# The first loads of a decoder layer spread over three DMA queues, and two of the first products exchanged

## The chip, the cores and the metric

The kernel runs on one core of one Trainium2 chip. The metric is the device time of one execution in microseconds, as the median of several runs.

## The reference

One layer of a decoder trunk works on x of 256 positions by 1024 channels, in float32. Cut to what matters here:

```python
h = rmsnorm(x, norm1_g)
u = einsum('bsd,de->bse', h, w_in)
x_rnn, g_rnn, q, k, v, g_br = split(u)        # 1024 columns each, g_br has 2048
ya = rg_lru(causal_dwconv(x_rnn)) * gelu(g_rnn)
yb = attention(rmsnorm(q), rmsnorm(k), v)     # 8 heads of 128, causal
x  = x + (sigmoid(gA) * (ya @ w_proj_rnn) + sigmoid(gB) * (yb @ w_proj_attn)) @ w_out
h  = rmsnorm(x, norm2_g)
x  = x + (gelu(causal_dwconv3(h @ w_up)) * (h @ w_gate)) @ w_down
```

The change touches only the beginning: the loads of x and of the columns of `w_in` that make k, and the first of the products x · w.

## The kernel before

Every float32 operand is split into a high part in the format that TensorE multiplies at full rate (fp32r) and a low part that holds the rest, and every product is made of three: high·high, high·low and low·high. ScalarE makes the high part (a cast for weights; for x an activation that also multiplies by the norm's factor g, tile `g1`), VectorE the low part (a subtraction). So nothing can be multiplied before its load has landed, ScalarE has cast it and, for the low parts, VectorE has subtracted.

TensorE works through units: `k` first, then `rx`, `rg`, `ri`, `q` and so on to `w_down`. In unit `k` the sum runs over eight slices of 128 channels, k = 0 to 7. For each slice there are two halves of 512 output columns, g = 0 and 1, and for each half three pairs of matmuls (a pair is the two halves of the 256 positions). So a slice is six pairs. Nine small matmuls on a tile of ones (`warm`) run before the first of them.

The first operands come in small pieces. `load_x(a, b)` loads slices a to b of x transposed into `xT` (128 KB a slice). `load_w(k, g)` loads 128 channels by 512 columns of weights into `raws` (256 KB). In the text x0, x1, x23 are the pieces of x for slice 0, slice 1 and slices 2 and 3, and w0.1 is the weight piece of slice 0, half 1. A piece of `raws` gives `his` and `los`; a slice of `xT` gives `xgh` and `xgl`. In unit `k`, SyncE's queue carries all pieces of x and of weights; ScalarE's queue carries only `g1`, of 4 KB.

Each engine takes its instructions strictly as they were issued. The order is written out by hand in the table `ORDER`: its numbers are non-matrix instructions in the order in which the program made them, and `+n` stands for the next n matmuls. `Later.issue` replays it. All instructions thus come from one line, L238, and the profile is read by the names of tiles.

After x and the weights of unit `k` comes a stream of 1 MB weight chunks (`raw`, split into `hi` and `lo`), each loaded some chunks ahead.

Of the kernel before, what the change touches and what calls it, by code (L numbers as in the profile page):

```python
# [17 lines left out]
KT = D // P  # L18
# [8 lines left out]
V_CW, V_CB, V_BR, V_BI, V_LAM, V_QG, V_KG, V_G1, V_FW, V_FB, V_G2 = 0, 32, 40, 48, 56, 64, 65, 66, 74, 140, 162  # L27
# [84 lines left out]
}  # L112

ORDER = """
0 4 1 3 26 28 30 32 2 29 31 +2 5 33-34 +1 7 37-38 6 35-36 +2 8 39-40 +1 10 43-44 9 41-42 +3 47-48 11 45-46 12 49-50 13
51-52 +5 15 55-56 +5 14 53-54 +13 16 59-60 57-58 18 63 17 65-66 64 61-62 19 67-68 +5 23 74-77 +3 20 224-226 69 24 27
227 25 228-235 71 105-106 236-242 +58 93 72 108 21-22 78 109 79-91 +1 96 +5 99 +37 73 142-143 92 102 95 97 94 117-118
120 119 121-122 243 123-126 244 127-133 +9 110 +3 111-112 101 103-104 187-188 107 190 +9 141 +5 116 115 113-114 98 100
# [123 lines left out]
def trunk_layer(ctx: ExitStack, tc: tile.TileContext, xT, x, vec, win_fm, win_tm, wri, wpr, wpa,  # L242
                wout, wup, wgate, wdown, out):
    nc = Later(tc.nc)
# [18 lines left out]
    def kt(t):  # L263
        return t.rearrange("p (k t) -> p k t", t=S)
# [46 lines left out]
    for u in FFN:  # L311
        kind, n = u[:2], int(u[2:])
# [40 lines left out]
    def advance(i):  # L353
        while ptr["split"] <= min(i, last):
            while ptr["load"] <= min(ptr["split"] + AHEAD_L, last):
                load_next()
            j = split_tiles()
            src = stream[j]
            n = 2048 if isinstance(src, list) else min(2048, src.shape[-1] * (2 if len(src.shape) == 3 else 1))
            m = {4: 2}.get(j, 1)  # L360
            for a in range(m):
                split_part(j, slice(a * n // m, (a + 1) * n // m), j in DVE_HI)
# [20 lines left out]
    def bank(name):  # L383
        return psB.tile([P, 512], F32, tag="B", name=name)
# [37 lines left out]

    xTs = Act("xT")
    g1 = const.tile([P, KT], F32, name="g1")
    nc.scalar.dma_start(g1, vec[:, V_G1:V_G1 + KT])
    ones = const.tile([P, P], F32, name="ones")
    nc.vector.memset(ones, 1.0)
    warm = bank("warm")
# [17 lines left out]
    ptr["load"] = ptr["split"] = START  # L446
    xs = const.tile([P, 2, D], F32, name="xs")

    def load_x(a, b):
        nc.sync.dma_start(kt(xTs.half(a // 4))[:, a % 4:a % 4 + b - a, :], xT[:, a:b, :])  # L450

    def load_w(k, g, n=1):
        d = praw[k // 2, g] if n == 2 else sraw[k, g]
        nc.sync.dma_start(d, win_tm[4 + 2 * g + k // 4, :, k % 4 * 512:(k % 4 + n) * 512])


    load_x(0, 1)
    load_w(0, 0)
    nc.scalar.preload_act_table(AF.Exp)
    load_w(0, 1)  # L460
    for k, n in ((1, 1), (2, 2), (4, 2), (6, 2)):
        load_x(k, k + n)
        for j in range(k, k + n, 2 if k > 3 else 1):
            for g in range(2):
                load_w(j, g, 2 if k > 3 else 1)
    pv = const.tile([P, V_N], F32, name="pv")
    nc.sync.dma_start(pv, vec)
    for t in range(2):
# [36 lines left out]
    xgh, xgl = Act("xgh", F32R), Act("xgl", F32R)  # L505
    def split_x(k):
        g = g1[:, k:k + 1]
        nc.scalar.activation(xgh[k], xTs[k], AF.Copy, scale=g)
        return lambda: nc.vector.scalar_tensor_tensor(xgl[k], xTs[k], g, f(xgh[k]), op0=OP.mult, op1=OP.subtract)

    def split_w(r, h, l, e=nc.scalar.copy):
        e(h, r)
        return lambda: nc.vector.tensor_sub(l, r, f(h))

    x = split_x(0)
    w = split_w(sraw[0, 0], shi[0, 0], slo[0, 0], nc.vector.tensor_copy)
# [89 lines left out]
    def ri(h, i, n4):  # L606
        wh = hi[i][:, :1024].rearrange("p (g n d) -> p g n d", g=2, n=4)
        wl = lo[i][:, :1024].rearrange("p (g n d) -> p g n d", g=2, n=4)
        n = 4 * h + n4
        ps = fm_ps(f"ri{n}")  # L610
        for g in range(2):
            mm3(ps[:, g, :], wh[:, g, n4, :], wl[:, g, n4, :], xah[n], xal[n], True, True)
        for g, dst, v in ((0, rt, V_BR), (1, it, V_BI)):
            nc.scalar.activation(dst[n], ps[:, g, :], AF.Sigmoid, bias=pv[:, v + n:v + n + 1])
# [30 lines left out]
    def tm_mm(ps, i, k, k4, ah, al, split=False, stat=lambda a, k, t: a[k][:, t * P:(t + 1) * P], ts=(0, 1)):  # L645


        at = (lambda a: a.rearrange("p (c k n) -> p k c n", c=2, k=4)[:, k4]) if split else (
            lambda a: a[:, k4 * 512:(k4 + 1) * 512])
        for t in ts:  # L650
            o = ps[t].rearrange("p (c n) -> p c n", c=2) if split else ps[t]
            mm3(o, stat(ah, k, t), stat(al, k, t), at(hi[i]), at(lo[i]), k == 0, k == KT - 1)
# [12 lines left out]
    def qk_evac(n, g, ps):  # L665


        if n == "k":
            r = raws[n, g] = half(f"{n}r{g}").rearrange("p (t c) -> p t c", t=2)
        v = ssq[n, g]  # L670
        for t in range(2):
            sq = small(f"sq{n}{g}{t}", 512)
            nc.scalar.activation(sq, ps[t], AF.Square, scale=rs1[:, t:t + 1])
            if n == "k":
                nc.scalar.copy(r[:, t, :], ps[t])
            nc.vector.reduce_sum(v[:, t], blk(sq), axis=AX.X)
        if n == "q":
            raws[n, g] = half(f"qd{g}")
            turn(f"qm{g}", raws[n, g], ps, f"rq{g}")
# [181 lines left out]
    def run_unit(kind, c):  # L861

        i = chunk[kind, c]
        if kind == "k":

            for g in range(2):
                k_ps[g] = [psA.tile([P, 512], F32, tag="A", name=f"k{g}{t}") for t in range(2)]
            for k in range(KT):
                for g in range(2):
                    for n, (x, w) in enumerate(((xgh, shi), (xgl, shi), (xgh, slo))):  # L870
                        for t in range(2):
                            nc.tensor.matmul(k_ps[g][t], x[k][:, t * P:(t + 1) * P], w[k, g], start=k == n == 0,
                                             stop=k == KT - 1 and n == 2)
            yield
            return
        advance(i)
        if kind == "ri":
            for n4 in range(4):
                ri(c, i, n4)
                yield  # L880
        else:
            g, kh = c // 2, c % 2
            if not kh:
                open_ps[kind, g] = [bank(f"{kind}{g}{t}") if kind in ("pa", "rx") else
                                 psA.tile([P, 512], F32, tag="A", name=f"{kind}{g}{t}") for t in range(2)]
            ps = open_ps[kind, g]
            args = (*{"pr": (yah, yal), "pa": (ybh, ybl), "wo": (mh, ml)}.get(kind, (xgh, xgl)),
                    kind not in ("q", "v", "wo"), *((m_stat,) if kind == "wo" else ()))
            if (kind, c) == ("wo", 1):

                for q in range(4):
                    for k4 in (2 * (q % 2), 2 * (q % 2) + 1):
                        tm_mm(ps, i, 4 * kh + k4, k4, *args, ts=(q // 2,))
                    if q % 2:
                        norm2_tile(q // 2, ps[q // 2])
                    yield
                return
            for k4 in range(4):
                tm_mm(ps, i, 4 * kh + k4, k4, *args)
                if kh and k4 == 3:  # L900
                    evac[kind](g, ps) if kind in evac else qk_evac(kind, g, ps)
                yield
# [86 lines left out]
    def norm2_tile(t, ps):  # L989

        x_ = xs[:, t, halves[0]]
        nc.vector.tensor_add(x_, ps, x_)
        if t:
            return
        turn_tile("hm0", turned_h0, x_, mid_h0, t)
        for k in range(4):
            d = blocks(turned_h0, t)[:, k]
            v = lambda a: a[k][:, t * P:(t + 1) * P].rearrange("p (i b) -> p i b", i=4)
            g = pv[:, V_G2 + k:V_G2 + k + 1]
            nc.scalar.activation(v(h2h), d, AF.Copy, scale=g)  # L1000
            nc.vector.scalar_tensor_tensor(v(h2l), d, g, f(v(h2h)), op0=OP.mult, op1=OP.subtract)
        squares(t, 0)
# [3 lines left out]
    for kind, c in units:  # L1006
        if (kind, c) not in (("k", 1), ("k", 2), ("k", 3)):
            run(f"{kind}{c}", run_unit(kind, c))
# [234 lines left out]
    for u in FFN[8:-1]:  # L1243
        kind, n, kh = u[:2], int(u[2]), int(u[3])
        if kind == "dn":
            j = int(u[2:])
# [13 lines left out]
    j = 9  # L1260
# [81 lines left out]
```

## Time and profile before

| what | value |
|---|---|
| median of 3 runs | 420.74 us (420.3 to 420.89) |
| span of the profiled execution, first to last instruction | 418.6 us |
| what the median holds beyond that span | 2.1 us |
| TensorE busy | 414.0 us (99%) |
| VectorE, ScalarE, GpSimd busy | 360.9, 307.5, 61.0 us |
| first matmul of unit `k` | starts at 5.16 us |
| DMA traffic | 106.89 MB, mean 255 GB/s |

The page gives no time of the profiled execution apart from its span, so changes are reckoned on the span and carried to the median. In a timeline row the columns are the start, the length, the engine, the operation, out<-in and the count of merged instructions, and in brackets the idle time ahead of it with what ended it. An engine's name with a q (SPq, ACTq) is its instruction queue, where DMA issues are seen; a DMA row "us to landing" runs from the issue until the whole piece is in place.

### The profile page before, as it was taken

What the parts mean: (1) busy time and instruction counts of PE and PEld (TensorE: products, weight loads), DVE (VectorE), ACT (ScalarE), POOL (GpSimd) and SP (SyncE); (2) the same over time, 40 slices, a digit from 0 to 9 for tenths busy, and PEclk for the clock granted to TensorE, in tenths of its full rate; (3) what the DMA queues carried; (4) which work ended last, traced back from release to release, by engine and by line L of the source; (5) the groups of instructions that cost most, each with busy time, mean ns of one, the idle gap of its engine ahead of it and who ended that gap; (6) DMA issues with size and microseconds to landing.
All of it is one profiled execution on the core that took longest, in us unless ns stands there. A gap on an engine that the chain in (4) does not pass through costs nothing.

```text
span 418.6 us, 5425 instructions
## 1 busy us (share of the span) xinstructions
PE 414.0 (99%) x1892; PEld 344.4 (82%) x1892; DVE 360.9 (86%) x449; ACT 307.5 (73%) x399; POOL 61.0 (15%) x109
## 2 busy tenths in 40 slices
PE   8999999999999999999999999999999999999996
PEld 7888888888888888888888888888888888888885
DVE  4877699999999999879896789899999989988863
ACT  4787478799989998796144475699897779866630
POOL 0084780009382002000000000000000000000000
PEclk9999999999999999999999999999999999999999
DMA  7998688979696988797698669575799748649803
GB/s 230 416 397 280 194 258 266 321 241 365 220 317 236 279 277 289 221 357 256 205 353 281 233 200 315 173 219 171 258 328 317 279 152 267 205 148 267 318 2 102
DMA packets 46108, 106.89 MB, mean 255 GB/s; under 512 B 8448, under 2 KB 22656, under 8 KB 43648
## 3 DMA queue, kind: packets, MB, share of 16 engines
q1 hardware_dynamic: 45360, 106.01, 76.1%
q10 hardware_dynamic: 720, 0.53, 0.4%
q8 instruction: 15, 0.25, 0.2%
q14 instruction: 13, 0.11, 0.1%
HBM read 92.63 MB, written 13.89 MB: 254 GB/s over the span
## 4 chain that ended last, share of the span: by engine, by line
PE 98%; DMA 1%; ACT 0%; DVE 0%; SPq 0%; issue 0%; ACTq 0%
PE acc L238 14%; PE up L238 13%; PE k L238 5%; PE gb L238 5%; PE qA L238 5%; PE pr L238 5%; PE wo L238 5%; PE ga L238 5%; PE v L238 5%; PE q L238 5%; PE pa L238 5%; PE rg L238 5%; PE rx L238 5%; PE qC L238 3%; PE gt L238 3%; PE last L238 3%
## 5 line engine op out<-in xcount | busy, mean ns | idle before, releaser
L238 DVE TENSOR_TENSOR lo<-raw,hi 128x2048 fp32r<-128x2048 f32 (+1 forms) x64 | 141.4, 2215 | 9.2 <-ACT hi L238 8.3
L238 ACT CAST hi<-raw 128x2048 fp32r<-128x2048 f32 (+1 forms) x64 | 118.2, 1856 | 29.2 <-DMA raw<-in_wout 16.7
L238 PE MATMUL up<-hi,h2l 128*128 128x512 f32 x80 | 31.1, 389 | 0.0
L238 PE MATMUL up<-hi,h2h 128*128 128x512 f32 x80 | 31.1, 389 | 0.0
L238 PE MATMUL up<-lo,h2h 128*128 128x512 f32 x80 | 31.1, 389 | 0.0
L238 PE MATMUL acc<-hi,fah 128*128 128x512 f32 x78 | 30.4, 390 | 0.0
L238 PE MATMUL acc<-hi,fal 128*128 128x512 f32 x78 | 30.4, 389 | 0.0
L238 PE MATMUL acc<-lo,fah 128*128 128x512 f32 x78 | 30.4, 389 | 0.0
L238 POOL TENSOR_TENSOR rsq<-rsq 128x8 f32<-128x8 f32 x32 | 21.0, 655 | 46.7 <-DVE rsq L238 44.5
L238 ACT ACT_TABLE_LOAD x14 | 18.0, 1283 | 1.4 <-PEq L1332 1.2
L238 PEld LDWEIGHTS up<-hi,h2h 128*128 128x128 f32 x80 | 15.0, 188 | 3.2
L238 PEld LDWEIGHTS up<-hi,h2l 128*128 128x128 f32 x80 | 15.0, 188 | 3.1
L238 PEld LDWEIGHTS up<-lo,h2h 128*128 128x128 f32 x80 | 15.0, 188 | 3.1
L238 PEld LDWEIGHTS acc<-hi,fah 128*128 128x128 f32 x78 | 14.6, 188 | 3.1
L238 PEld LDWEIGHTS acc<-lo,fah 128*128 128x128 f32 x78 | 14.6, 188 | 3.1
L238 PEld LDWEIGHTS acc<-hi,fal 128*128 128x128 f32 x78 | 14.7, 188 | 3.1
L238 DVE TENSOR_TENSOR loq<-wq,hiq 128x1024 fp32r<-128x1024 f32 x12 | 14.5, 1215 | 1.3 <-ACT hiq L238 1.3
L238 ACT ACTIVATE fu<-fupd,pv 128x256 f32<-128x256 f32 x32 | 15.2, 502 | 0.5 <-DVE fc L238 0.3
L238 ACT CAST hiq<-wq 128x1024 fp32r<-128x1024 f32 x12 | 12.3, 1049 | 4.1 <-PE acc L238 2.2
L238 DVE TENSOR_TENSOR wq<-wq,wq 128x1024 f32<-128x1024 f32 x12 | 14.6, 1216 | 0.2
L238 DVE TENSOR_TENSOR lot<-wq,hit 128x1024 fp32r<-128x1024 f32 x12 | 14.4, 1218 | 0.0
L238 ACT CAST hit<-wq 128x1024 fp32r<-128x1024 f32 x12 | 12.2, 1045 | 1.0 <-PE acc L238 1.0
(303 smaller groups left out, 1175.3 us busy)
## 6 DMA issues: line engine op xcount, KB each, us to landing
raw<-in_win_fm SPq DMA_DIRECT2D x16, 1024.0 KB, 7.0
raw<-in_wdown SPq DMA_DIRECT2D x11, 1024.0 KB, 6.1
raw<-in_wup SPq DMA_DIRECT2D x10, 1024.0 KB, 5.9
raw<-in_win_tm SPq DMA_DIRECT2D x8, 1024.0 KB, 6.7
wq<-in_wgate SPq DMA_DIRECT2D x16, 512.0 KB, 6.2
raw<-in_wpr SPq DMA_DIRECT2D x4, 1024.0 KB, 7.6
raw<-in_wpa SPq DMA_DIRECT2D x4, 1024.0 KB, 7.8
raw<-in_wout SPq DMA_DIRECT2D x8, 512.0 KB, 5.4
```

What stands on the lines that cost most here:

```text
L238: getattr(engine, name)(*map(real, a), **{n: real(v) for n, v in k.items()})
```

## The change

Three things change, all in the first microseconds.

- x0 is now the first piece on SyncE's queue. The pieces w0.0, x1 and w1.0 go out on ScalarE's queue, ahead of its table load.
- `g1` goes out on GpSimd's queue, ahead of GpSimd's mask.
- For slice 0, half 0 alone, the pair with the weights' low part comes before the pair with x's low part.

```diff
 ORDER = """
-0 4 1 3 26 28 30 32 2 29 31 +2 5 33-34 +1 7 37-38 6 35-36 +2 8 39-40 +1 10 43-44 9 41-42 +3 47-48 11 45-46 12 49-50 13
+0 2 3 6 7 1 4 26 28 30 32 29 31 5 +2 33-34 +1 37-38 35-36 +2 8 39-40 +1 10 43-44 9 41-42 +3 47-48 11 45-46 12 49-50 13
...
-    nc.scalar.dma_start(g1, vec[:, V_G1:V_G1 + KT])
+    nc.gpsimd.dma_start(g1, vec[:, V_G1:V_G1 + KT])
...
-    def load_x(a, b):
-        nc.sync.dma_start(kt(xTs.half(a // 4))[:, a % 4:a % 4 + b - a, :], xT[:, a:b, :])
+    def load_x(a, b, e=nc.sync):
+        e.dma_start(kt(xTs.half(a // 4))[:, a % 4:a % 4 + b - a, :], xT[:, a:b, :])
-    def load_w(k, g, n=1):
+    def load_w(k, g, n=1, e=nc.sync):
         d = praw[k // 2, g] if n == 2 else sraw[k, g]
-        nc.sync.dma_start(d, win_tm[4 + 2 * g + k // 4, :, k % 4 * 512:(k % 4 + n) * 512])
+        e.dma_start(d, win_tm[4 + 2 * g + k // 4, :, k % 4 * 512:(k % 4 + n) * 512])
     load_x(0, 1)
-    load_w(0, 0)
+    load_w(0, 0, e=nc.scalar)
     nc.scalar.preload_act_table(AF.Exp)
     load_w(0, 1)
     for k, n in ((1, 1), (2, 2), (4, 2), (6, 2)):
-        load_x(k, k + n)
+        load_x(k, k + n, nc.scalar if k == 1 else nc.sync)
         for j in range(k, k + n, 2 if k > 3 else 1):
             for g in range(2):
-                load_w(j, g, 2 if k > 3 else 1)
+                load_w(j, g, 2 if k > 3 else 1, nc.scalar if (j, g) == (1, 0) else nc.sync)
...
-                    for n, (x, w) in enumerate(((xgh, shi), (xgl, shi), (xgh, slo))):
+                    for n, (x, w) in enumerate(((xgh, shi), *((xgl, shi), (xgh, slo))[::-1 if k == g == 0 else 1])):
```

On SyncE, at the program's start, these rows stood before. The `raws` rows are w0.0, then w0.1 and w1.0, then w1.1, then w2.0; the `xT` rows are x0, x1 and x23. A number behind an underscore only tells buffers apart.

```order
L238 DMA raws_82<-in_win_tm 128x512
L238 DMA xT_93<-in_xT 128x256
L238 DMA raws_82<-in_win_tm 128x512 x2
L238 DMA xT_93<-in_xT 128x256
L238 DMA raws_82<-in_win_tm 128x512
L238 DMA raws_118<-in_win_tm 128x512
L238 DMA xT_93<-in_xT 128x512
```

At the same place on SyncE now: x0, then w0.1 and w1.1, then w2.0, then x23.

```order
L238 DMA xT_79<-in_xT 128x256
L238 DMA raws_81<-in_win_tm 128x512 x2
L238 DMA raws_118<-in_win_tm 128x512
L238 DMA xT_79<-in_xT 128x512
L238 DMA raws_118<-in_win_tm 128x512 x3
```

Three pieces have left the queue, and what stays has kept its order but for x0, which leads.

On ScalarE, at the program's start, the difference is this. The casts are `his` of w0.1 and w1.0 (x2), and of w1.1; the activations are `xgh` of slices 0 and 1.

```order
-L238 DMA g_77<-in_vec 128x8
-L238 ACT_TABLE_LOAD
-L238 ACTIVATE xgh_95<-xT_93,g_77 128x256
-L238 CAST his_89<-raws_82 128x512 x2
-L238 ACTIVATE xgh_95<-xT_93,g_77 128x256
-L238 CAST his_89<-raws_82 128x512
+L238 DMA raws_81<-in_win_tm 128x512
+L238 DMA xT_79<-in_xT 128x256
+L238 DMA raws_81<-in_win_tm 128x512
+L238 ACT_TABLE_LOAD
+L238 ACTIVATE xgh_97<-xT_79,g_77 128x256
+L238 CAST his_93<-raws_81 128x512 x2
```

Three DMA issues (w0.0, x1, w1.0) take the place of one; what ScalarE computes stands in the same order as before: x0, w0.1, w1.0, x1, w1.1.

## Prediction

> **What bounds the kernel now.** I read the page first, its engines.
>
> ```profile
> span 418.6 us, 5425 instructions
> PE 414.0 (99%) x1892; PEld 344.4 (82%) x1892; DVE 360.9 (86%) x449; ACT 307.5 (73%) x399; POOL 61.0 (15%) x109
> ```
>
> TensorE is busy 414.0 of 418.6 us. So a change that leaves its work alone can only move the 4.6 us that are left. The chain of work that ended last, in order of time, shows where they lie:
>
> ```profile
> 1.17 3.34 DMA xT<-in_xT
> ...
> 4.60 0.52 ACT xgh L238
> ...
> 5.16 22.51 PE k L238 x96
> ...
> 414.02 1.44 PE end L238 x12
> ```
>
> The chain passes from x0's load (issued 1.17, landed 4.51) over ScalarE's product with g to TensorE at 5.16, and never leaves TensorE until the end. Whatever shifts the stream of matmuls in the first microseconds shifts the end by as much. The start itself is next, in the timeline of TensorE:
>
> ```profile
> 1.03 3.68 PE L238 MATMUL warm<-ones 128*128 128x128 f32 x18 [1.03 <-DVE ones L238]
> 5.16 0.73 PE L238 MATMUL k<-his,xgh 128*128 128x512 f32 x2 [0.45 <-ACT xgh L238]
> 5.80 0.73 PE L238 MATMUL k<-his,xgl 128*128 128x512 f32 x2
> 6.37 0.63 PE L238 MATMUL k<-los,xgh 128*128 128x512 f32 x2
> 6.90 0.73 PE L238 MATMUL k<-his,xgh 128*128 128x512 f32 x2
> 7.47 0.62 PE L238 MATMUL k<-his,xgl 128*128 128x512 f32 x2
> 7.92 0.62 PE L238 MATMUL k<-los,xgh 128*128 128x512 f32 x2
> 8.38 0.62 PE L238 MATMUL k<-his,xgh 128*128 128x512 f32 x2
> ...
> 10.96 0.38 PEld L238 LDWEIGHTS k<-his,xgh 128*128 128x128 f32 x2
> 11.15 0.63 PE L238 MATMUL k<-his,xgh 128*128 128x512 f32 x2
> ```
>
> Pairs that wait for nothing start 0.46 us apart (7.92 to 8.38); the pair behind one that had waited starts 0.57 after it (6.90 to 7.47). Warm-ups end at 4.71, so the first pair can gain 0.45 at most. With nothing late after that, slice 2 would start at 4.71 + 0.57 + 11 × 0.46, about 10.3, where it now starts at 11.15: 0.85 us is all that this change can win. Slice 1 starts at 8.38 and slice 2 at 11.15, and they are where I check the supply. ScalarE and VectorE there:
>
> ```profile
> 0.71 0.41 ACTq L238 DMA_DIRECT2D g<-in_vec  x1
> 1.15 1.28 ACT L238 ACT_TABLE_LOAD   x1 [1.15 <-PEq L1332]
> 4.60 0.51 ACT L238 ACTIVATE xgh<-xT,g 128x256 fp32r<-128x256 f32 x1 [2.16 <-DMA xT<-in_xT]
> 6.23 1.14 ACT L238 CAST his<-raws 128x512 fp32r<-128x512 f32 x2 [1.12 <-DMA raws<-in_win_tm]
> 7.40 0.51 ACT L238 ACTIVATE xgh<-xT,g 128x256 fp32r<-128x256 f32 x1
> 8.05 0.62 ACT L238 CAST his<-raws 128x512 fp32r<-128x512 f32 x1
> 10.40 0.91 ACT L238 ACTIVATE xgh<-xT,g 128x256 fp32r<-128x256 f32 x2 [0.97 <-DMA xT<-in_xT]
> ```
> ```profile
> 4.20 0.43 DVE L238 CAST his<-raws 128x512 fp32r<-128x512 f32 x1 [3.22 <-DMA raws<-in_win_tm]
> 4.66 0.69 DVE L238 TENSOR_TENSOR los<-raws,his 128x512 fp32r<-128x512 f32 x1
> 5.27 0.48 DVE L238 SCALAR_TENSOR_TENSOR xgl<-xT,g,xgh 128x256 fp32r<-128x256 f32 x1
> ```
>
> Slice 2's first product stands right behind its x: `xgh` starts at 10.40 when x23 lands, ends 0.51 later at 10.91, and its weights are loaded at 10.96. There is no slack, so a gain at the front is lost again at slice 2, but for under 0.2 us, unless x23 lands earlier too. The first wait is not the one that decides; the supply by DMA is.
>
> The loads, from the DMA view (sizes in KB, us from issue to landing; the rows are g1, w0.0, x0 and x23) and two of SyncE's issues, x1 and then w1.1 with w2.0:
>
> ```profile
> g<-in_vec ACTq DMA_DIRECT2D x1, 4.0 KB, 3.6
> raws<-in_win_tm SPq DMA_DIRECT2D x1, 256.0 KB, 3.5
> xT<-in_xT SPq DMA_DIRECT2D x1, 128.0 KB, 3.3
> xT<-in_xT SPq DMA_DIRECT2D x1, 256.0 KB, 6.0
> ```
> ```profile
> 2.58 0.43 SPq L238 DMA_DIRECT2D xT<-in_xT  x1
> 3.05 0.91 SPq L238 DMA_DIRECT2D raws<-in_win_tm  x2
> ```
>
> A piece is issued every 0.45 us, and w1.1, issued at 3.05, lands when ScalarE casts it at 8.05: five microseconds of backlog. The 16 DMA engines limit, not the issuing. Two counts show how they share themselves between queues. The first is g1's whole transfer, the second the half microsecond from 2.0 to 2.5:
>
> ```profile
> q10 hardware_dynamic: 144, 0.00, 0.2%
> ...
> q1 hardware_dynamic: 22, 0.05, 26.6%
> q10 hardware_dynamic: 18, 0.00, 2.0%
> ```
>
> A piece is 128 rows, one packet each, and 16 closing packets (144), so eight rows on each engine. From 2.0 to 2.5 SyncE's queue (q1) and ScalarE's (q10) moved 22 and 18 packets, though q1's have 2 KB and q10's 32 bytes. They take turns packet by packet; that is why 4 KB of g1 needed 3.6 us beside 256 KB that needed 3.5.
>
> **The change part by part.** *Three pieces on ScalarE's queue.* Before, with all in one line, the KB moved by the time each piece is whole, and its landing: w0.0 256 (4.2), x0 384 (4.5), w0.1 640 (6.2), x1 1024 (7.4), w1.1 1280 (8.05), x23 1792 (10.4). w1.0, at 896, was cast behind w0.1 without a pause (6.23, 1.14 for two) and ended at 7.37; its own 0.62 before that it had landed, by 6.75. Now two lines take turns, eight rows to a piece: x0 with w0.0 are whole at 384, w0.1 with x1 at 768, w1.1 with w1.0 at 1280, then w2.0 and x23 at 1792 as before. On the same clock of bytes that is 4.5, about 6.5 (between 640 at 6.2 and 896 at 6.75), 8.05 and 10.4. So x0 gains nothing, w0.0 comes 0.3 later, x1 0.9 earlier, and **w1.0 1.3 later**. ScalarE takes w1.0 ahead of x1, so x1's early landing is of no use.
>
> The stream by these landings. First pair: `xgh` of x0 still ends at 5.11, first pair at 5.16, no gain. Slice 0, half 1: w0.1 at 6.5, cast 0.62, pair at 7.15 (before 6.90). Slice 1: w1.0 at 8.05, cast 0.62 to 8.67, `xgh` 0.51 to 9.2, pair at 9.25 (before 8.38). VectorE: `los` of w1.0 0.69 from 8.70, then `xgl` 0.48 to 9.9, second pair at 9.93 rather than 9.82; third at 10.50; the three of half 1 follow at 0.46, and slice 2 starts at 12.34. Against 11.15 that is **+1.2 us**. x23 at 10.4 is then ready in time, and no later piece is behind its old place on the clock of bytes.
>
> *What could be earlier.* A second line may fill gaps. The stretches, with the DMA share and GB/s last in the row:
>
> ```profile
> 2.00:3.00 1.00, 1.00 (x7) 1.00 (x6) 0.00 (x0) 0.44 (x1) 0.00 (x0) 1.00 0.60 172
> 5.16:8.38 3.22, 3.22 (x13) 2.21 (x13) 2.09 (x5) 1.99 (x4) 0.00 (x0) 1.00 1.02 305
> 11.15:27.51 16.36, 16.36 (x73) 13.47 (x72) 12.48 (x16) 12.54 (x18) 5.39 (x13) 1.00 1.03 416
> ```
>
> Only the ramp has gaps: 0.60 busy from 2 to 3, so at most 0.4 us. I credit half, 0.2 us, since an engine that has not got its first descriptor cannot use a second line; the ends are 0 and 0.4. The Trainium skill ("DMA: Bandwidth & Descriptors", "Issuing engines are not separate DMA queues") says that issuing from several engines saves only the issuing time. By that the credit is 0 and the sum +1.2.
>
> *Exchanged pairs.* VectorE has `los` ready 0.69 after its cast and `xgl` 0.48 after that. With w0.0 at 4.5, `los` ends near 5.7, in time for 5.73, and `xgl` at 6.2. The second pair starts 0.07 earlier than its 5.80 of now, the third 0.14 earlier than 6.37; both run up against w0.1 at 7.15. Worth 0.
>
> *ScalarE's issues.* Two more at 0.41 to 0.45 put the table load at about 2.1 to 3.4, ahead of 4.5. Cost 0, covered by ScalarE's wait of 2.16; without that cover, 0.9.
>
> *g1 on GpSimd.* No row shows a load from there. Its own landing on ScalarE's queue is 3.6 after issue; the slowest first piece took 6.0, so g1 lands between 4.3 and 6.7; earlier buys nothing, since x0 comes at 4.5. The stream stands until about 5.8: `xgh` to 6.35, `his` of w0.1 to 6.97, slice 1 still waits for w1.0. I take the near row, 0; the far one costs 0.9. GpSimd's mask behind it is covered:
>
> ```profile
> 21.41 0.27 POOL L238 TENSOR_SCALAR decw<-pv 128x8 f32<-128x8 f32 x1 [19.91 <-DMA pv<-in_vec]
> ```
>
> GpSimd idles 19.91 us after its mask.
>
> *Sum.* +1.2 − 0.2 = +1.0 us on the span of 418.6, that is 419.6. The median of the runs, 420.74, holds 2.1 us beyond the span that the change doesn't touch: **421.74**.
>
> **The rivals.** A (forecast): packet turns, w1.0 lands near 7.9; own range 421.3 to 422.1.
>
> B: turns of a whole piece, w1.0 ahead of w1.1, whole at 1024 KB (7.4). Slice 1 then starts at 8.63, its second pair at 9.30 behind `xgl`, slice 2 at 11.7: +0.55, 421.3. The counts 22 and 18 speak against it. The Trainium skill (same page, "Queues, rings and completion order") lets an engine drain a packet of some 9 to 17 descriptors from one queue before it turns; by that, eight rows would go in one turn, and B holds instead of A. This trace's rows count single rows in turn.
>
> C: the early rate, 305 GB/s, was the one queue's own limit, and two reach the 416 of later. The 896 KB after 384 then need 2.15 us: w1.0 at 6.65, x23 at 7.9. Slice 1 starts at 8.07, bound by the first pair at 5.16, slice 2 at 10.8: −0.3, 420.4. The DMA share of 1.02 speaks against it: the engines were occupied.
>
> D: g1 comes at 6.7 or later: +0.9 on top, 422.6. First use of a path is what speaks for it.
>
> F, the other side: the second line feeds the engines from their first packet, x0 and w0.0 land by 4.1, the first pair follows the warm-ups at 4.71. It decides only if x23 also lands by about 9.5: −0.85, 419.9.
>
> **How the numbers follow.** A measurement of this kernel can tell about 0.2%, 0.84 us. A 0.58, of which 0.12 lies under +0.84 and counts as the same; B 0.15, same; C 0.14, same; D 0.09, slower; F 0.04, faster. Slower 0.46 + 0.09 = 0.55, same 0.12 + 0.15 + 0.14 = 0.41, faster 0.04. The range reaches down into C at 420.4 and up to 422.4, short of D: F, half of C, and most of D are left out, under 0.2.
>
> **What would show it.** Right: ScalarE's second `his` cast starts near 7.9, not 6.75, with a wait for `raws`; TensorE's first pair of slice 1 near 9.1, slice 2 near 12.1; w1.0 lands together with w1.1. The first pair stays within 0.2 of 5.16. Wrong: slice 2 at or under 11.15 with x23 landing well under 10.4 (C or F); `xgh` of x0 released by `g` and not `xT` (D).

## The result, and the profile after

The changed kernel takes 425.51 us, the median of 4 runs (424.74 to 426.03), against 420.78 before on the same chip: a ratio of 1.0113 [1.0098, 1.0127], 4.7 us slower. The prediction said 421.74. Its profiled execution, the slowest of the four, took 426.03 us, of which the span is 424.3; so 1.7 us lie beyond the span, and the 2.1 used in the forecast set the median of three runs against the span of one. Two executions among all the runs behind this text (one of the kernel before, one of an experiment), of 461 us at a mean clock of 0.85, stand apart from the rest and are left out of every figure. The page first:

```profile
span 424.3 us, 5426 instructions
PE 416.5 (98%) x1892; PEld 346.7 (82%) x1892; DVE 361.0 (85%) x449; ACT 307.6 (73%) x399; POOL 57.6 (14%) x110
PEclk8899999999999999999999999999999999999999
```

The span grew by 5.7 us, TensorE's busy time by 2.5. So TensorE does not only wait longer, it also works more slowly somewhere, and the clock row says where: its first two of 40 slices show an 8. The chain of work that ended last, in order of time (start, length, what):

```profile
1.22 6.43 DMA g<-in_vec
...
7.67 0.52 ACT xgh L238
...
8.23 24.95 PE k L238 x96
```

It no longer passes through x0's load but through `g1`'s, 4 KB that needed 6.43 us. Unit `k` begins 3.07 us later than before (8.23 for 5.16) and takes 2.44 us longer (24.95 for 22.51). These two make 5.5 of the 5.7 us. TensorE in the timeline:

```profile
1.04 3.73 PE L238 MATMUL warm<-ones 128*128 128x128 f32 x18 [1.04 <-DVE ones L238]
8.23 1.22 PE L238 MATMUL k<-his,xgh 128*128 128x512 f32 x2 [3.46 <-ACT xgh L238]
9.25 1.05 PE L238 MATMUL k<-los,xgh 128*128 128x512 f32 x2
...
13.52 1.02 PE L238 MATMUL k<-his,xgh 128*128 128x512 f32 x2
14.37 0.64 PE L238 MATMUL k<-his,xgl 128*128 128x512 f32 x2
14.85 0.63 PE L238 MATMUL k<-los,xgh 128*128 128x512 f32 x2
```

After 3.46 us of idleness the pairs start 0.85 us apart, not 0.46, until 14.37. GpSimd and ScalarE there, in the timeline, show the wait:

```profile
1.22 0.78 POOL L238 DMA_DIRECT2D g<-in_vec  x1 [0.79 <-POOLq L1332]
```
```profile
2.13 1.28 ACT L238 ACT_TABLE_LOAD   x1 [2.13 <-issue]
7.67 0.51 ACT L238 ACTIVATE xgh<-xT,g 128x256 fp32r<-128x256 f32 x1 [4.25 <-DMA g<-in_vec]
...
8.96 0.62 ACT L238 CAST his<-raws 128x512 fp32r<-128x512 f32 x1 [0.27 <-DMA raws<-in_win_tm]
```

The DMA issues (KB each, us from issue to landing) are x0, w0.0, `g1`, w1.1 and w1.0:

```profile
xT<-in_xT SPq DMA_DIRECT2D x1, 128.0 KB, 3.1
raws<-in_win_tm ACTq DMA_DIRECT2D x1, 256.0 KB, 3.3
g<-in_vec POOLq DMA_DIRECT2D x1, 4.0 KB, 6.4
...
raws<-in_win_tm SPq DMA_DIRECT2D x1, 256.0 KB, 7.1
raws<-in_win_tm ACTq DMA_DIRECT2D x1, 256.0 KB, 7.3
```

x0 and w0.0, issued at 0.72, had landed by 4.0. VectorE, which makes the high part of this one piece, cast w0.0 at 4.07, but ScalarE held x0 back, and with it the first pair, until 7.67 for the factor that it multiplies with. w1.1 and w1.0 landed at about 8.7 and 8.95, so w1.0 was late too; but behind `g1` that cost its cast a wait of only 0.27 us.

### The profile page after: what moved, and what is told of

Same layout as the page of the kernel before. It is cut to its first block, busy times and chain, and to the rows that moved or that the text cites. A ratio compares the mean times of both kernels' runs of the same rounds, so it can differ in the third digit from the quotient of the medians.

```text
span 424.3 us, 5426 instructions
## 1 busy us (share of the span) xinstructions
PE 416.5 (98%) x1892; PEld 346.7 (82%) x1892; DVE 361.0 (85%) x449; ACT 307.6 (73%) x399; POOL 57.6 (14%) x110
## 4 chain that ended last, share of the span: by engine, by line
PE 97%; DMA 2%; issue 0%; ACT 0%; DVE 0%; POOLq 0%
PE acc L238 14%; PE up L238 13%; PE k L238 6%; PE gb L238 5%; PE qA L238 5%; PE pr L238 5%; PE wo L238 5%; PE ga L238 5%; PE v L238 5%; PE q L238 5%; PE pa L238 5%; PE rg L238 5%; PE rx L238 5%; PE qC L238 3%; PE gt L238 3%; PE last L238 3%
## 5 line engine op out<-in xcount | busy, mean ns | idle before, releaser
L238 PE MATMUL k<-his,xgh 128*128 128x512 f32 x32 | 11.3, 438 | 3.5 <-ACT xgh L238 3.5
L238 DVE TENSOR_TENSOR lot<-wq,hit 128x1024 fp32r<-128x1024 f32 x12 | 14.4, 1219 | 0.0
```

The lines of the kernel that those rows point to most:

```text
L238: getattr(engine, name)(*map(real, a), **{n: real(v) for n, v in k.items()})
```

## The experiments

Three theories could explain the loss, and they add up in different ways. First, `g1` comes late from GpSimd's queue. Second, the idle time that this causes halves TensorE's clock. Third, the two hardware queues take turns, which delays w1.0; this is what the prediction rested on. Rivals were the exchanged pairs and the place of x0 ahead of w0.0. The table gives each run's profile (first pair, start of slice 2, span) and its ratio to before:

| kernel | first pair | slice 2 | span | median | ratio |
|---|---|---|---|---|---|
| before | 5.16 | 11.15 | 418.6 | 420.61 to 420.78 | 1 |
| after | 8.23 | 16.70 | 424.3 | 425.51 | 1.0113 [1.0098, 1.0127] |
| after, `g1` on ScalarE | 6.83 | 12.91 | 420.3 | 422.21 | 1.0043 [1.0031, 1.0056] |
| before, `g1` on GpSimd | 5.48 | 11.80 | 419.4 | 421.13 | 1.0020 [1.0003, 1.0036] |
| after, 17 warm-ups | 8.26 | 13.83 | 421.4 | 423.08 | 1.0056 [1.0043, 1.0070] |
| before, pairs exchanged | 5.18 | 11.64 | 419.1 | 420.86 | 1.0003 [0.9994, 1.0012] |
| after, `g1` inside x0 | 5.53 | 12.64 | 420.1 | 421.97 | 1.0034 [1.0022, 1.0046] |
| after, one piece on ScalarE | 5.98 | 13.43 | 421.0 | 422.09 | 1.0038 [1.0024, 1.0052] |
| `g1` inside x0, one piece on ScalarE | 4.96 | 10.72 | 418.2 | 420.41 | 0.9997 [0.9988, 1.0006] |
| before, x0 ahead of w0.0 | 5.43 | 11.59 | 419.0 | 420.89 | 1.0012 [1.0003, 1.0020] |
| after, two pieces later | 8.02 | 15.17 | 422.7 | 425.02 | 1.0101 [1.0083, 1.0118] |
| `g1` inside x0, one piece, 7 warm-ups | 4.88 | 11.00 | 418.5 | 420.31 | 0.9999 [0.9987, 1.0011] |

In every row the span stands from before's as slice 2 does, within 0.2 us. What happens ahead of slice 2 decides all of it. Each row's profile is one execution, and a difference of half a microsecond between two rows can be the execution alone: single runs of the kernel before took 420.22 to 421.23 us.

### More warm-ups: the clock by itself

Eight more small matmuls keep TensorE busy while `g1` is awaited.

```diff
-HALVES, SMALLS, WARM, RAWS = 23, 10, 9, 3
+HALVES, SMALLS, WARM, RAWS = 23, 10, 17, 3
-0 2 3 6 7 1 4 26 28 30 32 29 31 5 +2 33-34 ...
+0 2 3 6 7 1 4 26 28 30 32 29 31 5 +10 33-34 ...
```

> The changed kernel with 17 small warm-up matmuls rather than 9, so that they last until about 8 us. Theory 1a (of the loss, 3.1 us is the wait for g1 and the rest is the halved clock that follows 3.5 us of idle TensorE): the granted clock stays at full, unit k takes 22.5 us rather than 24.95, 423.0 to 423.8 us. Rival (products at the start are slow because their operands come late, whatever the clock): pairs still 0.85 us apart from 9 to 14 us, 425 to 426 us.

TensorE in that run's timeline:

```profile
1.04 6.11 PE L238 MATMUL warm<-ones 128*128 128x128 f32 x34 [1.04 <-DVE ones L238]
8.26 0.73 PE L238 MATMUL k<-his,xgh 128*128 128x512 f32 x2 [1.11 <-ACT xgh L238]
8.82 0.62 PE L238 MATMUL k<-los,xgh 128*128 128x512 f32 x2
```

The stretch from 7.5 to 14.4 us in three kernels, from the view by stretches (from, to, length, then PE, PEld, DVE, ACT, POOL busy; granted clock, DMA share and GB/s last): before, after, and this run.

```profile
7.50:14.40 6.90, 6.90 (x32) 5.59 (x31) 5.23 (x10) 5.05 (x9) 0.00 (x0) 1.00 1.01 378
```
```profile
7.50:14.40 6.90, 6.17 (x15) 4.82 (x16) 5.97 (x11) 6.07 (x12) 0.00 (x0) 0.51 1.03 394
```
```profile
7.50:14.40 6.90, 6.14 (x27) 5.10 (x28) 6.00 (x12) 6.40 (x12) 0.00 (x0) 1.00 1.00 358
```

The first pair starts where it did (8.26), the idle time is 1.11 rather than 3.46 us, and the granted clock is 1.00 rather than 0.51: 27 matmuls fit where 15 did. The median falls by 2.4 us (425.51 to 423.08), unit `k` by 2.9 in the records (24.95 to 22.05). So half of the loss is the clock. The Trainium skill ("TensorE: Matmul & The Clock Gate", Part 1) says that about 3.4 us of idleness halve TensorE's clock and about 3.4 us of work restore it. This case's trace differs a little: read in steps of 0.1 us, the clock column falls at about 7.55, 2.8 us after the last warm-up ended (4.77) and before the first pair began, and it rises at about 14.35, 6.1 us after the first pair began.

The fall itself is shown for the profiled run only. The mean clock of the four timed runs was 0.992 (the profiled one; 6.8 us at half pace in 424.3 give just that), 1.000, 0.995 and 0.999, so two of them show no such fall, though they took 425.60 and 425.42 us. A start at half pace while the column reads 1.00 does occur, as the run with one piece on ScalarE shows below; no trace shows whether it occurred in these two. What the longer warm-ups show for the median is that a busy TensorE is spared the 2.4 us.

The other 2.3 us (1.0056) are the wait itself. It put the first pair back by 3.1 us, and unit `k` won 0.46 of that back (22.05 for 22.51), since its operands had gathered meanwhile.

### `g1` back on ScalarE's queue

```diff
-    nc.gpsimd.dma_start(g1, vec[:, V_G1:V_G1 + KT])
+    nc.scalar.dma_start(g1, vec[:, V_G1:V_G1 + KT])
```

> The changed kernel, but the norm's factors g1 go out on ScalarE's queue again, as its first load, ahead of w0.0, x1 and w1.0. Theory 1 (g1's late landing from GpSimd is the whole loss, and taking turns between the two queues costs nothing): 420.3 to 420.9 us, first product at 4.7 to 5.2, slice 2 at 11.2 or earlier. Theory 2 (g1 hid the loss that was forecast: w1.0 lands with w1.1 near 8 us and holds up slice 1): 421.3 to 422.1 us, first product near 5.2, slice 1 near 9.2, slice 2 near 12.2.

The run took 1.0043, not as little as the queue order alone should cost; its 422.21 us lie above the range of either theory. Its chain:

```profile
1.16 5.07 DMA raws<-in_win_tm
...
6.26 0.44 DVE his L238
...
6.83 22.56 PE k L238 x96
```

`g1` landed in time, but w0.0, now behind it on the queue, landed at 6.23 rather than 4.0. The packets from 1.7 to 2.7 us, in the DMA view:

```profile
q1 hardware_dynamic: 127, 0.12, 48.2%
q10 hardware_dynamic: 92, 0.00, 4.9%
```

SyncE's queue (q1) moved 127 packets and 0.12 MB; ScalarE's (q10) moved 92, nearly as many, but they were `g1`'s and held nothing to speak of; in the changed kernel the same queue moved 0.11 MB of w0.0 in this microsecond. If turns go row by row, eight rows of 32 bytes on each engine cost w0.0 as many turns as eight rows of 2 KB would, and the counts fit that. They do not prove it: the engines were busy for only 53% of this microsecond, so something besides their being full held w0.0 back. The run therefore did not isolate the queue order; it showed that a small load ahead of a large one in the same queue is not small.

### `g1` inside x0's piece: the queue order by itself

The host's array puts the eight factors of a channel ahead of its row of x0, so one load brings both, and neither GpSimd's queue nor extra rows are needed. A one-column memset on GpSimd stands in for the dropped load, so that the numbers of `ORDER` still fit. All else, but for that memset's place in `ORDER`, is as in the changed kernel.

```diff
-    nc.gpsimd.dma_start(g1, vec[:, V_G1:V_G1 + KT])
+    xg0 = const.tile([P, KT + S], F32, name="xg0")
+    g1 = xg0[:, :KT]
+    nc.sync.dma_start(xg0, xg)
...
-    load_x(0, 1)
+    nc.gpsimd.memset(const.tile([P, 1], F32, name="idle"), 0.0)
...
-        g = g1[:, k:k + 1]
+        g, x_ = g1[:, k:k + 1], xTs[k] if k else xg0[:, KT:]
```

> The changed kernel with its three pieces on ScalarE's queue and its exchanged pairs, but g1 comes inside x0's piece (8 more columns in front of its 256), so no load of g1 is left. Theory 2 (w1.0 waits its turn beside w1.1 and is late; that loss was there under the loss by g1): first product near 4.7, ScalarE's cast of w1.0 near 8 us, slice 1 near 9.2, slice 2 near 12.1, 421.4 to 422.1 us. Rival (without g1's lateness the changed queues gain): slice 2 at 11.0 or earlier, 420.6 us or less.

Chain, then TensorE's timeline:

```profile
1.64 6.77 DMA raws<-in_win_tm
...
8.44 0.62 ACT his L238
9.06 0.42 ACT xgh L238
...
9.52 19.60 PE k L238 x84
```
```profile
5.53 0.70 PE L238 MATMUL k<-his,xgh 128*128 128x512 f32 x2 [0.55 <-DVE his L238]
...
7.74 0.72 PE L238 MATMUL k<-his,xgh 128*128 128x512 f32 x2 [0.38 <-ACT his L238]
...
9.52 0.74 PE L238 MATMUL k<-his,xgh 128*128 128x512 f32 x2
...
12.64 0.61 PE L238 MATMUL k<-his,xgh 128*128 128x512 f32 x2
```

This is the forecast's mechanism, row by row. The chain passes through w1.0 (landed 8.42, before by 6.75), its cast, `xgh` of slice 1 and slice 1's first pair; slice 2 starts at 12.64. The cost is 1.28 us in the medians (421.97 and 420.69), within the range expected, though the rows came later than expected: w0.0 landed only at 4.9, so the first pair stood at 5.53 rather than 4.7. The kernel before differs from this one also in how `g1` comes. Against the run further below that differs in x1 and w1.0 alone (`g1` inside x0, one piece on ScalarE, 420.41), the two pieces cost 1.56 us. So `g1` on GpSimd, with what follows from it, accounts for the remaining 3.5 of the changed kernel's 4.7 us (425.51 less 421.97).

### How late `g1` comes from GpSimd

Two runs vary what else is queued. The first is the kernel before with `g1` alone moved, so that ScalarE's queue is empty:

```diff
-    nc.scalar.dma_start(g1, vec[:, V_G1:V_G1 + KT])
+    nc.gpsimd.dma_start(g1, vec[:, V_G1:V_G1 + KT])
```

> The kernel before, with one change: g1 goes out on GpSimd's queue. Theory 1 (g1's late landing is the whole loss): 425 to 426 us, g1 lands near 7.6 us with ScalarE's wait put down to it, first product near 8.2, the clock falls to half for a while. Rival (the load from GpSimd is late only because three queues share the DMA engines): with ScalarE's queue empty g1 lands by 5.5 us, and the time is 421.5 us or less.

The second is the changed kernel with only w0.0 on ScalarE's queue (x1 and w1.0, and what ScalarE computes from them, stand in `ORDER` as they did before):

```diff
-        load_x(k, k + n, nc.scalar if k == 1 else nc.sync)
+        load_x(k, k + n)
...
-                load_w(j, g, 2 if k > 3 else 1, nc.scalar if (j, g) == (1, 0) else nc.sync)
+                load_w(j, g, 2 if k > 3 else 1)
```

> The changed kernel, but only w0.0 stays on ScalarE's queue; x1 and w1.0 go back to SyncE's, in the order of the kernel before. g1 stays on GpSimd's queue. Theory 3 (g1's packets wait behind the pieces that wait on the two other queues; the more pieces on ScalarE's, the later): g1 lands between 4.9 us (seen with ScalarE's queue empty) and 7.65 us (seen with three pieces), near 6 us, 421 to 423 us. Rival a (any big piece on a third queue delays it fully): 7.5 us or later, 424 to 426 us. Rival b (one piece does no harm): 5.0 us or earlier, 421 us or less.

The two chains, in that order:

```profile
1.22 3.68 DMA g<-in_vec
...
5.48 22.80 PE k L238 x96
```
```profile
1.23 4.17 DMA g<-in_vec
...
5.98 23.94 PE k L238 x96
```

Issued at the same time in all three, the same 4 KB needed 3.68 us with ScalarE's queue empty, 4.17 with one piece on it and, in the changed kernel, 6.43 with three. Moving `g1` alone costs 0.35 us in the medians (421.13 for 420.78); the ratio of 1.0020 is 0.8 us, since three of its ten runs took 422.9 to 423.1. So the rival held there (`g1` at 4.9, under 421.5 us), and theory 3 in the second run (`g1` at 5.4, 422.09 us).

The second run lost more than its first pair shows (1.0038), and TensorE's timeline and the same stretch of it say why:

```profile
5.98 1.22 PE L238 MATMUL k<-his,xgh 128*128 128x512 f32 x2 [0.73 <-ACT xgh L238]
7.00 1.05 PE L238 MATMUL k<-los,xgh 128*128 128x512 f32 x2
...
9.56 0.84 PE L238 MATMUL k<-his,xgl 128*128 128x512 f32 x2
10.24 0.62 PE L238 MATMUL k<-los,xgh 128*128 128x512 f32 x2
```
```profile
7.50:14.40 6.90, 6.90 (x27) 5.55 (x26) 4.77 (x10) 4.78 (x9) 0.00 (x0) 1.00 0.98 368
```

The pairs stand 0.85 apart up to 9.56, the pace of the halved clock, though the clock column says 1.00. In this run the clock had not risen at all before: its warm-ups too took 4.21 us, where the same eighteen records took 3.68 in the kernel before. The column, which shows a fall, does not show the first rise; in the run with more warm-ups 7 warm-up records ran between 3 and 4 us and 10 between 5 and 6, and it reads 1.00 in both. The pace of the pairs is the better witness at a program's start. The four runs of this kernel took 421.4 twice, 422.8 (the one profiled) and 423.1; whether the first two had an earlier rise is not shown.

### Two pieces later on ScalarE

To learn whether the pieces queued ahead of `g1` or the later ones delay it, x1 and w1.0 were written behind the table load.

```diff
-0 2 3 6 7 1 4 26 28 30 32 29 31 5 +2 33-34 ...
+0 2 3 1 4 6 7 26 28 30 32 29 31 5 +2 33-34 ...
```

> The changed kernel, but ScalarE issues x1 and w1.0 behind its table load, at 2.45 us and later rather than 1.16; GpSimd's load of g1 has ended its issue at 2.0 us, so only w0.0 is in ScalarE's queue by then. Theory 3a (g1 waits for the pieces that stood in the queues when its own packets were made): g1 lands near 5.4 us, as with one piece, 421.5 to 422.5 us. Theory 3b (g1 waits as long as both other queues stay busy, whenever their pieces came): g1 lands at 7 us or later, 424 to 426 us.

ScalarE's timeline, the chain's step for `g1`, TensorE's first pair, and the stretch from 7.5 us:

```profile
1.17 1.28 ACT L238 ACT_TABLE_LOAD   x1 [1.17 <-PEq L1332]
1.20 0.42 ACTq L238 DMA_DIRECT2D xT<-in_xT  x1
1.65 0.45 ACTq L238 DMA_DIRECT2D raws<-in_win_tm  x1
```
```profile
1.23 6.21 DMA g<-in_vec
```
```profile
8.02 1.06 PE L238 MATMUL k<-his,xgh 128*128 128x512 f32 x2 [2.92 <-ACT xgh L238]
```
```profile
7.50:14.40 6.90, 6.38 (x21) 5.14 (x22) 6.07 (x11) 6.39 (x12) 0.00 (x0) 0.75 0.98 330
```

The experiment did not do what it was meant to. The issues ran beside the table load, at 1.20 and 1.65, as early as in the changed kernel; `g1` landed at 7.4 and the time stayed (1.0101). What holds back GpSimd's packets is therefore open. The run was still of use for the clock: TensorE idled 2.92 us here, and the clock was halved too, from about 8.25 to 11.65. So 2.92 us can be enough, under the Trainium skill's 3.4, and 1.11 (the run with more warm-ups) was not. The half pace lasted 3.4 us here and 6.8 in the changed kernel, once and twice the same length, so what a wait costs by the clock does not follow from its length alone.

### The exchanged pairs, and x0 ahead of w0.0

Each was done alone on the kernel before.

```diff
-                    for n, (x, w) in enumerate(((xgh, shi), (xgl, shi), (xgh, slo))):
+                    for n, (x, w) in enumerate(((xgh, shi), *((xgl, shi), (xgh, slo))[::-1 if k == g == 0 else 1])):
```

> The kernel before, with one change: for slice 0, half 0, the pair with the weights' low part comes ahead of the pair with x's low part. Both theories: 420.5 to 420.9 us; second and third pair each about 0.1 us earlier, then both run up against the cast of w0.1, which starts at 6.2.

```diff
-0 4 1 3 26 28 30 32 2 29 31 +2 5 33-34 ...
+0 4 1 2 26 28 29 3 30 32 31 +2 5 33-34 ...
```

> The kernel before with one change: x0 goes out ahead of w0.0 on SyncE's queue; g1 stays alone on ScalarE's. Both theories: x0 lands near 3.7, w0.0 near 4.5 (before 4.5 and 4.2), first product near 5.0, and slice 2 is set by x23 as before: 420.5 to 421.0 us.

The pairs cost nothing (1.0003 [0.9994, 1.0012]). x0 ahead alone costs 0.1% (1.0012 [1.0003, 1.0020]): x0 lands early, but w0.0 only at 4.83, and the first pair waits for w0.0 instead (5.43 for 5.16). Neither explains the loss. The rows expected did not all come: with the pairs exchanged the first pair ran at half pace, so the second stood at 6.20 (5.80 before) and slice 2 at 11.64; with x0 ahead x23 landed by 9.89, and slice 2, at 11.59, did not wait for it.

### What the change can be worth without its two costs

`g1` inside x0's piece, only w0.0 on ScalarE's queue, the pairs exchanged (an edit of the run with `g1` inside x0, with the casts and the first matmuls in the order of the run with one piece on ScalarE); then the same with 7 warm-ups, for which `ORDER` loses two matmuls too.

```diff
-        load_x(k, k + n, nc.scalar if k == 1 else nc.sync)
+        load_x(k, k + n)
...
-                load_w(j, g, 2 if k > 3 else 1, nc.scalar if (j, g) == (1, 0) else nc.sync)
+                load_w(j, g, 2 if k > 3 else 1)
```

> As the run with g1 inside x0's piece, but only w0.0 is on ScalarE's queue; the other pieces are on SyncE's in the order of the kernel before. Theory 2: the pieces come in the order in which they are used, x0 and w0.0 land near 4.0 together, first product at 4.7, w0.1 and w1.0 no later than before, x23 lands by 10.2: 420.2 to 420.6 us, 0.2 to 0.5 us faster than before. Rival (the second wait takes all of it back): 420.7 to 420.9 us.

```diff
-HALVES, SMALLS, WARM, RAWS = 23, 10, 9, 3
+HALVES, SMALLS, WARM, RAWS = 23, 10, 7, 3
```

> As the run with g1 inside x0's piece and only w0.0 on ScalarE's queue, with 7 warm-up matmuls rather than 9, so that they end about 0.5 us earlier. If the first product stands behind the warm-ups there: first product near 4.75, 420.0 to 420.4 us. Rival (the clock then rises later, and what is won at the front is lost to slow products): 420.4 to 421.0 us.

With 9 warm-ups, TensorE in the timeline:

```profile
1.03 4.21 PE L238 MATMUL warm<-ones 128*128 128x128 f32 x18 [1.03 <-DVE ones L238]
4.96 0.88 PE L238 MATMUL k<-his,xgh 128*128 128x512 f32 x2
...
10.72 0.61 PE L238 MATMUL k<-his,xgh 128*128 128x512 f32 x2
```

The stream now follows the warm-ups without a gap, and slice 2 starts 0.43 us earlier than before (10.72 for 11.15). Over all runs that is nothing that can be measured (0.9997 [0.9988, 1.0006]), and seven warm-ups change nothing either (0.9999 [0.9987, 1.0011]), though both medians lie in the ranges expected. Single runs spread from 419.97 to 420.90 us with nine warm-ups and from 419.94 to 422.20 with seven; so what is left to win here is less than what one run differs from the next.

The loads did come earlier here. With nine warm-ups w0.1 landed by 5.06 and x23 by 8.82 (6.2 and 10.40 before; x23 by 9.74 with seven); by 6 us 1.25 MB had moved, against 1.04 before and 0.95 in the run with three pieces on ScalarE's queue. So the second queue, with the rows of `g1` gone, can fill the ramp with one piece on it and not with three; why is open.

## Why the prediction was wrong, point by point

**What bounds the kernel** held. TensorE's stream from slice 2 on is the same in every kernel, and only the start moves the end.

**Three pieces on ScalarE's queue, +1.2:** right in mechanism and near in size, as the run with `g1` inside x0 shows: +1.28 us, with w1.0 landed at 8.42 (forecast 8.05), slice 1 at 9.52 (9.25 without the credit) and slice 2 at 12.64 (12.34). The pieces ahead of it were as late against the forecast: w0.0 4.9 for 4.5, w0.1 7.07 for 6.5. In the changed kernel it is invisible. There w1.0 landed with w1.1, as foretold, but the wait for `g1` put the stream back so far that w1.0 had landed before its pair was due.

**The credit of 0.2** for gaps in the ramp did not come with three pieces on the second queue: 0.95 MB had moved by 6 us, less than the 1.04 before. The Trainium skill ("DMA: Bandwidth & Descriptors", "Issuing engines are not separate DMA queues") gave 0 for it, and the measured 1.28 agrees with the sum of 1.2 that the prediction worked out by that rule. One piece there does not fit the rule as well: of the two runs with `g1` on GpSimd, the one with w0.0 on ScalarE's queue had w0.1 landed at 5.2, the one with all pieces on SyncE's at 6.35, and the issue was only 0.47 us earlier.

**The exchanged pairs, 0, and ScalarE's issues, 0:** right. The table load stood at 2.13 to 3.41, as forecast, and ScalarE waited 4.25 us behind it.

**`g1` on GpSimd is the step that failed.** The prediction bounded its landing between 4.3 and 6.7, took the near end and wrote 0. It landed at 7.65, beyond the far end. Half of the overshoot is the issue: the bounds count from 0.71, where ScalarE had issued it, and GpSimd issued it at 1.22. The rest is the 6.43 us that it then took. Both bounds came from rows of the two hardware queues; no row of before showed GpSimd's queue, and how a third queue fares beside two busy ones does not follow from how one fares beside another. Rival D had the mechanism and its sign (`xgh` of x0 released by `g`), but it was priced with a landing at 6.7. Its 0.9 for the wait was too dear for that landing: with the clock held up, the whole start cost 2.3 us, 1.0 more than queue order alone, and this at a landing of 7.68.

**The clock was not in the sum at all.** A wait of 3.46 us on TensorE cost 2.4 us more by the halved pace behind it. D left TensorE idle from about 4.7 for over 2 us, and nothing in the prediction asked what its clock would do.

**Rivals B, C and F** did not occur. With turns of whole pieces (B), or with a faster early rate (C), slice 1 would have started at 8.63 or 8.07; with `g1` out of the way it started at 9.52. F's condition, x23 landed by about 9.5, was met only with one piece on ScalarE's queue, in some of its profiles (8.82 with `g1` inside x0). There the first pair stood at 4.96, not 4.71, since the warm-ups took longer (4.21 us for 3.68), and slice 2 gained 0.43, not 0.85 us.

The whole: 1.3 us by queue order, hidden under a wait that makes it 2.3, and 2.4 by the clock behind that wait, which gives the 4.7.

## What to carry to other kernels

Before a load moves to another queue, ask who waits for its last byte: a 4 KB table of factors that the first instruction needs is worth more care than 256 KB of weights, and can ride inside the piece that is needed with it. Spreading pieces over queues changes the order in which they are whole, so reckon each landing by turns and not by issue alone; here three pieces on a second queue made the needed one land later (8.42 for 6.75), while one piece there did no harm. Price a wait on TensorE at the head of a stream twice, once for the time and once for the clock that falls when the wait is long.

## What the runs showed of the hardware that was not expected

- GpSimd's queue moved `g1` as 32 packets, where ScalarE's queue needed 144. The after page's queue row:

```profile
q0 software_dynamic: 32, 0.00, 0.0%
```

- Few packets did not make it quick: 3.7, 4.2 and 6.4 us from issue to landing beside none, one and three pieces on ScalarE's queue. GpSimd's issue itself took only 0.78 us in all three. Why the third queue's packets wait so long is open.
- An issue written behind a table load on ScalarE does not wait for it (1.20 beside 1.17 to 2.45).
- The clock at the program's start rises at moments that differ among kernels whose warm-ups start alike: the pairs ran at full pace from the first on (5.53) in the run with `g1` inside x0, and only from near 10 us in the run with one piece on ScalarE. No experiment here controls that moment. It may differ among runs of one kernel too, since the single times of several fall into two groups about 1.5 to 2 us apart (`g1` alone moved: seven of 420.5 to 421.2, three of 422.9 to 423.1), but no kernel was profiled in both.
